# First mixture of experts: the rows of units 4 to 13 by DRAM and indirect gathers that add onto h

## The chip, the cores and the metric

The kernel runs on one core of a Trainium2 chip. The metric is the time of one execution on the device in microseconds, as a median of runs. The profile shows one further execution, taken by the hardware profiler.

## The reference

Two blocks run one after the other on 512 tokens of 1024 numbers in float32. Each is a mixer (two kinds of attention or recurrence side by side), an addition to h, a mixture of experts, and another addition to h. The change lies in the mixture of the first block. Each token chooses one of 4 groups, and 2 of the 8 experts of that group:

```python
def hier_moe(x2d, w_grp, b_grp, w_exp, b_exp, w_gate, w_up, w_down):
    ...
    combine = jnp.sum(jax.nn.one_hot(global_idx, N_EXPERTS, dtype=jnp.float32) * weights[..., None], axis=1)
    y = jnp.zeros_like(x2d)
    for e in range(N_EXPERTS):
        h = jax.nn.silu(x2d @ w_gate[e]) * (x2d @ w_up[e])
        y = y + combine[:, e:e + 1] * (h @ w_down[e])
    return y
...
        h = h + y.reshape(B, S, D)
```

There are 32 experts. `w_gate` and `w_up` are 1024 x 256 each, `w_down` is 256 x 1024: 3 MB an expert in float32.

## The kernel before

**Units.** The first mixture (`moe1`, lines 1626 to 1734) computes only the chosen pairs of token and expert. Each expert has 64 slots; a unit is two experts, 128 slots on 128 partitions, so there are 16 units. The routing, ahead of it, writes the normalised tokens to DRAM (xd) and makes a table of the token number of each slot. For a unit, GpSimd (POOL) gathers the tokens by an indirect transfer (L1579, xg<-xd,idx), TensorE (PE) transposes them (L1592), and multiplies them with the gate and up weights of the two experts: the hidden layer, 64 products that each use half of the columns of PE (L1673). ScalarE (ACT) and VectorE (DVE) make silu(gate) * up, PE transposes that (L1718, `turned`), and the down-projection follows: 16 products (L1641) into two banks of PSUM. ACT and DVE multiply the rows with the slots' weights and split them in a high and a low part (L1738, L1739, `rows_hl`).

**The scatter.** The rows of the slots have to reach the rows of h, which stays in SBUF as four tiles of 128 tokens. Before the change all units do so by products: DVE makes a one-hot matrix of slot and token (L1743), PE multiplies it with the high and the low parts (L1759, L1760: per unit 4 tiles x 2 halves x 2 parts = 16 products), and DVE adds the result onto h (L1753). Two units are summed in PSUM, and their scatter is spread over two later units, half of the columns in each.

**The order.** A unit's down-projection is written after the hidden layer of the next unit. The tile scheduler orders the instructions of each engine ahead of time. After unit 15's hidden layer stands a loop for further rounds (`moe_rounds`, L1572), which handles experts with more than 64 tokens. With these inputs it runs zero times, but its branch is a barrier of all engines, and POOL's and SP's part of it waits until the transfers issued so far have landed. Behind it `end` runs the down-projection of unit 15, its scatter, and `sums_two` (from line 386), the start of the norms of the second block.

**The weights.** SP issues the 96 pieces of 1 MB in the order of use (L1523) into a ring of 17 places of four parts (0 to 3), as places come free. Three of the pieces are issued by POOL.

**Other names.** `places` (L1419) computes where a token's rows stand in DRAM; before the change it is called for the second mixture alone, which sends 14 of its 16 units by a DRAM array yd (stores at L1828) and reads the rows back by plain gathers (L1885). In the first mixer `g` (L470) is a part of the small "lora" weights, `w` the pieces of the input projection (L282), `qz` a tile whose upper half is zero. The mixer goes through steps written out by hand: R for the recurrence, P for projections, A for attention.

## Time and profile before

| what | us |
|---|---|
| runs: lowest, median, highest | 1439.62, 1442.21, 1443.59 |
| span of the profiled execution | 1440.1 |
| PE busy in it | 1329.5 (92%) |
| first mixture, first hidden layer to the last addition onto h | 466.5 to 747.9 |
| the loop's branch on SP | 730.4 |

The page gives the whole execution: busy time by engine, the span in 40 slices, the chain that ended last, and the groups of instructions that cost most. The trace behind it answers for any stretch: which engine was busy, which instruction waited for what, how long a transfer took from issue to landing. The number in front of a row of a timeline is its start, in microseconds from the start of the span.

### The profile page before, as it was taken

Reading aid. Unit: us, or ns where it says so; the run is one execution under the profiler, and the core shown is the slowest. Engines: PE = TensorE matmul, PEld = TensorE weight load, DVE = VectorE, ACT = ScalarE, POOL = GpSimd, SP = SyncE. Lnnn points to the kernel's source line nnn. Section 1 sums busy time; section 2 is a strip of 40 time slices with the busy share of each in tenths; the row PEclk is TensorE's granted clock in tenths of the full one; section 3 lists DMA queues with packets and bytes.
Section 4 is the critical chain, followed back from the end, with each engine's and each line's share of the span. In section 5 each row is a group of like instructions: output and inputs, shape, how many; then the busy total and the mean of one; then the engine's idle time right before and its main releaser. Section 6 shows DMA issues by size and latency. Waiting matters only on the chain. (4 is left out here: it accounts for less than half of the span.)

```text
span 1440.1 us, 20831 instructions
## 1 busy us (share of the span) xinstructions
PE 1329.5 (92%) x7952; PEld 954.6 (66%) x7952; DVE 891.8 (62%) x1498; ACT 700.5 (49%) x1217; POOL 390.2 (27%) x311
## 2 busy tenths in 40 slices
PE   7999999989997999999959899999896999999994
PEld 5776766757696556555528677767795666666662
DVE  4578856575745123323255847565747799999995
ACT  6433433333644212111144555555634788888883
POOL 1010224331104000000047201010223555555555
PEclk9999999999998999999989999999997999999997
DMA  5222100000584999998122111201385899889943
GB/s 186 74 88 74 52 16 1 1 1 2 226 325 166 407 422 422 422 417 346 42 74 72 59 47 57 73 31 34 130 356 199 280 367 373 320 339 395 380 177 147
DMA packets 49286, 273.53 MB, mean 190 GB/s; under 512 B 7497, under 2 KB 8393, under 8 KB 23570
## 3 DMA queue, kind: packets, MB, share of 16 engines
q1 hardware_dynamic: 41058, 249.48, 45.4%
q0 software_dynamic: 7248, 21.24, 4.2%
q10 hardware_dynamic: 864, 1.31, 0.3%
q8 instruction: 66, 1.08, 0.3%
q14 instruction: 50, 0.41, 0.1%
HBM read 266.48 MB, written 11.80 MB: 193 GB/s over the span
## 5 line engine op out<-in xcount | busy, mean ns | idle before, releaser
L1608 DVE TENSOR_TENSOR elo<-ew,ehi 128x1024 fp32r<-128x1024 f32 x147 | 231.3, 1615 | 31.9 <-ACT ehi L1607 23.1
L1607 ACT ACTIVATE ehi<-ew 128x1024 fp32r<-128x1024 f32 x192 | 203.0, 1060 | 61.8 <-PE ua L1855 42.3
L317 PE MATMUL mm<-xh,whi 128*128 128x512 f32 (+1 forms) x384 | 156.6, 408 | 4.0 <-DVE hq L1134 3.7
L317 PE MATMUL mm<-xh,wlo 128*128 128x512 f32 (+1 forms) x384 | 153.3, 399 | 0.0
L317 PE MATMUL mm<-xl,whi 128*128 128x512 f32 (+1 forms) x384 | 152.9, 398 | 0.5 <-DVE xl L349 0.3
L1608 POOL TENSOR_TENSOR elo<-ew,ehi 128x1024 fp32r<-128x1024 f32 x45 | 126.0, 2803 | 63.9 <-ACT ehi L1607 62.2
L1673 PE MATMUL mm<-ew,xTh 128*64 128x256 f32 x1024 | 120.0, 386 | 0.0
L1856 PE MATMUL ua<-elo,xTh 128*96 128x512 f32 x256 | 102.8, 402 | 8.4 <-DVE elo L1608 8.4
L1854 PE MATMUL ua<-ehi,xTh 128*96 128x512 f32 x256 | 101.9, 398 | 0.7 <-ACT xTh L1596 0.6
L1579 POOL DMA_INDIRECT xg<-xd,idx x32 | 36.6, 1145 | 242.7 <-PE sb L1592 153.3
L1855 PE MATMUL ua<-ehi,xTl 128*96 128x512 f32 x256 | 101.6, 397 | 0.0
L1673 PEld LDWEIGHTS mm<-ew,xTh 128*64 128x64 f32 x1024 | 73.6, 139 | 41.9 <-issue 8.0
L291 ACT ACTIVATE whi<-w 128x1024 fp32r<-128x1024 f32 x53 | 55.9, 1056 | 86.7 <-PE mm L317 68.0
L292 DVE TENSOR_TENSOR wlo<-w,whi 128x1024 fp32r<-128x1024 f32 x52 | 64.1, 1234 | 52.4 <-ACT whi L291 51.0
L317 PEld LDWEIGHTS mm<-xh,whi 128*128 128x128 f32 x384 | 73.8, 192 | 23.0 <-DVE hq L1134 5.3
L317 PEld LDWEIGHTS mm<-xl,whi 128*128 128x128 f32 x384 | 73.7, 192 | 16.3 <-issue 3.0
L317 PEld LDWEIGHTS mm<-xh,wlo 128*128 128x128 f32 x384 | 73.4, 191 | 16.3 <-issue 2.6
L1676 ACT ACTIVATE hh<-mm 128x256 f32<-128x256 f32 x16 | 6.1, 383 | 128.9 <-PE mm L1673 128.9
L1677 DVE TENSOR_TENSOR hh<-hh,mm 128x256 f32<-128x256 f32 x16 | 6.7, 421 | 95.1 <-ACT hh L1676 95.1
L1641 PE MATMUL ua<-ew,hT 128*64 128x512 f32 x240 | 65.3, 600 | 0.0
L1856 PEld LDWEIGHTS ua<-elo,xTh 128*96 128x96 f32 x256 | 41.8, 163 | 30.4 <-DVE elo L1608 11.2
L1738 ACT ACTIVATE oh<-ua,wts 128x512 fp32r<-128x512 f32 x30 | 20.6, 687 | 72.9 <-PE ua L1641 72.9
(632 smaller groups left out, 3160.9 us busy)
## 6 DMA issues: line engine op xcount, KB each, us to landing
ew<-in_e1up_dram SPq DMA_DIRECT2D x32, 1024.0 KB, 15.2
ew<-in_e2up_dram SPq DMA_DIRECT2D x32, 1024.0 KB, 11.2
ew<-in_e2gate_dram SPq DMA_DIRECT2D x32, 1024.0 KB, 9.9
ew<-in_e2down_dram SPq DMA_DIRECT2D x32, 1024.0 KB, 11.7
ew<-in_e1gate_dram SPq DMA_DIRECT2D x31, 1024.0 KB, 17.8
ew<-in_e1down_dram SPq DMA_DIRECT2D x30, 1024.0 KB, 16.3
w<-in_win_dram SPq DMA_DIRECT2D x53, 512.0 KB, 3.5
ew<-in_wout_dram SPq DMA_DIRECT2D x8, 1024.0 KB, 7.2
```

Source lines behind the costliest of these rows:

```text
L291: nc.scalar.activation(hi, s, AF.Copy)
L292: (eng or nc.vector).tensor_tensor(lo, s, hi, OP.subtract)
L317: mm = lambda w, x, start=False, stop=False: nc.tensor.matmul(p[:, s], w[:, k], x[:, k, s], start=start, stop=stop, skip_group_check=parts ...
L1579: return self.nc.gpsimd.indirect_dma_start(out=xg, out_offset=None, in_=mo.xd, in_offset=bass.IndirectOffsetOnAxis(ap=idx[:, u:u + 1], axi ...
L1607: self.hi = nc.scalar.activation(hi, s, AF.Copy)
L1608: self.lo = (nc.gpsimd if pool else nc.vector).tensor_tensor(lo, s, hi, OP.subtract)
L1641: nc.tensor.matmul(p[hs(a)], hT[:, k, hs(a)], w[a][:, k * 1024 + d * 512:k * 1024 + d * 512 + 512], start=k == 0, stop=k == 1)
L1673: nc.tensor.matmul(d[hs(a)], xT[:, k, hs(a)], w[2 * m + a][:, k * 256:k * 256 + 256], start=k == 0, stop=k == KD - 1)
L1738: self.last = self.nc.scalar.activation(oh, p, AF.Copy, scale=w)
L1854: nc.tensor.matmul(p, xh[:, kk], hi[:, s], start=kk == 0, stop=False)
L1855: nc.tensor.matmul(p, xl[:, kk], hi[:, s], start=False, stop=False)
L1856: nc.tensor.matmul(p, xh[:, kk], lo[:, s], start=False, stop=kk == KD - 1)
```

## The change

Units 4 to 13 (experts 8 to 27) no longer scatter by products. Their down-projections go through a new function `by_dram`: ACT multiplies the rows with their weights into a tile `ot` (two copies, no split), and POOL stores it by one indirect transfer to `yd`, an array of 1280 rows in DRAM; a slot without a token has a row number out of bounds, and its row is not stored. In unit 14, after unit 13's store, POOL issues eight indirect gathers which add the rows of yd onto h, one for each of the four tiles of tokens and each of a token's two experts (c = 0, 1). Tokens whose expert is not among the twenty have a row number out of bounds. Units 0 to 3 keep the one-hot products in units 3 to 6. Units 14 and 15 keep them too, summed in PSUM in `end` behind the loop: 32 products there instead of 16. `places` is now called in the first mixture as well, and also makes the row numbers of the stores. In step P2 of the first mixer one transfer of SP fills yd with zeros, 5.24 MB in rows of 2 KB. Tags of some tiles are merged, and two of the kept tiles share one place of the ring. In the order of PE, ACT, DVE and POOL in the first mixer some instructions near steps R2, A1 and P2 trade places; their number is the same.

The constants `row` and BYDRAM of the second mixture become `row2` and BYDRAM[2], with the same values. The core of the diff:

```diff
@@ -24,13 +24,16 @@
 SILU = "silu_and_others"
-BYDRAM = 14
-ZROW = BYDRAM * 96
+FROM = {1: 8, 2: 0}
+BYDRAM = {1: 20, 2: 14}
+CAP = {1: 64, 2: 96}
+ZROW = {k: BYDRAM[k] * CAP[k] for k in CAP}
 KAPPA = float(np.exp(-0.5))
@@ -59,8 +62,8 @@
     "mo": (("io64", 64), ("tok", 8), ("upb", 128)),
-    "mo1": (("cap64", 8), ("sl64", 128), ("g_f1", 8)),
-    "mo2": (("cap96", 8), ("sl96", 128), ("g_f2", 8), ("row", 16)),
+    "mo1": (("cap64", 8), ("sl64", 128), ("g_f1", 8), ("row1", 32), ("out1", 16)),
+    "mo2": (("cap96", 8), ("sl96", 128), ("g_f2", 8), ("row2", 16)),
 })
@@ -92,11 +95,13 @@
     put("g_f1", cols(inp["norm_ffn_g"]))
-    put("row", one * np.where(np.arange(16) < BYDRAM, 96 * np.arange(16), 1e5))
+    for k, e in (1, np.arange(32)), (2, np.arange(16)):
+        put("row%d" % k, one * np.where((e >= FROM[k]) & (e < FROM[k] + BYDRAM[k]), CAP[k] * (e - FROM[k]), 1e5))
+    put("out1", i[:, None] + 128 * np.arange(16) - CAP[1] * FROM[1])
     put("g_f2", cols(inp["ffn_norm_2"]))
@@ -487,11 +492,16 @@
                 qkv[j] = self.sb_proj(pp, sp, j, xh, xl)
+                if j == 2:
+                    self.yd = tc.dram_tile([ZROW[1], D], F32, name="yd1")
+                    zeros = qkv[j][0][64:128, 0]
+                    nc.sync.dma_start(self.yd.rearrange("(p a) (d c) -> p (a d) c", p=64, c=T),
+                                      zeros[:, None, :].to_broadcast([64, ZROW[1] // 32, T]))
                 if j == 3:
@@ -1011,10 +1021,9 @@
             self.totals(mo.rp, mo, lb[:, 0:mo.E])
-            if mo.which == 2:
-                self.places(mo.rp, mo)
-
+            self.places(mo.rp, mo)
     def mixer2(self, after):
@@ -1417,22 +1426,29 @@
         nc.vector.tensor_tensor(tm.rearrange("p n c e -> p (n c) e"), mo.M.rearrange("p n c e -> p (n c) e"),
-                                self.c("row")[:, None, :].to_broadcast([128, 2 * NT, E]), OP.mult)
+                                self.c("row%d" % mo.which)[:, None, :].to_broadcast([128, 2 * NT, E]), OP.mult)
         nc.vector.tensor_reduce(rw, tm, AX.X, OP.add)
...
         nc.vector.tensor_tensor(rw, rw, ov, OP.add)
-        nc.vector.tensor_scalar(mo.row, rw, float(ZROW), None, op0=OP.min)
+        if mo.which == 2:
+            nc.vector.tensor_scalar(mo.row, rw, float(ZROW[2]), None, op0=OP.min)
+            return
+        nc.vector.tensor_copy(mo.row, rw)
+        ot = rp.tile([128, mo.U], F32, name="rot")
+        nc.vector.tensor_scalar(ot, mo.num, 4096.0, 1e5, op0=OP.is_ge, op1=OP.mult)
+        nc.vector.tensor_tensor(mo.out, ot, self.c("out1"), OP.add)
 
@@ -1479,7 +1495,8 @@
         mo.extra = mo.keep.tile([1, 1], I32, name="extra")
-        mo.row = mo.keep.tile([128, NT, 2], I32, name="row") if which == 2 else None
+        mo.row = mo.keep.tile([128, NT, 2], I32, name="row")
+        mo.out = mo.keep.tile([128, mo.U], I32, name="out") if which == 1 else None
         self.upb = self.cbf(mo.keep, "upb")
@@ -1630,21 +1647,38 @@
 
-        def down(hT, w, wt, SC):
+        def product(hT, w, d):
+            p = self.ps("dn")
+            for k in range(2):
+                for a in range(2):
+                    nc.tensor.matmul(p[hs(a)], hT[:, k, hs(a)], w[a][:, k * 1024 + d * 512:k * 1024 + d * 512 + 512],
+                                     start=k == 0, stop=k == 1)
+            return p
+        def by_dram(u, hT):
+            w = [self.moe_next(mo) for _ in range(2)]
+            ot = yp.tile([128, D], F32, tag="o1", name="ot", bufs=3)
+            for d in range(2):
+                nc.scalar.activation(ot[:, 512 * d:512 * d + 512], product(hT, w, d), AF.Copy, scale=mo.wts[:, u:u + 1])
+            nc.gpsimd.indirect_dma_start(
+                out=self.yd, out_offset=bass.IndirectOffsetOnAxis(ap=mo.out[:, u:u + 1], axis=0), in_=ot, in_offset=None,
+                bounds_check=ZROW[1] - 1, oob_is_err=False)
+        def down(hT, w, wt, SC, at=None):
             hl = []
             for d in range(2):
-                hl.append([yp.tile([128, 512], R32, name=nm + str(d), bufs=2 + d) for nm in ("oh", "ol")])
-                p = self.ps("dn")
-                for k in range(2):
-                    for a in range(2):
-                        nc.tensor.matmul(p[hs(a)], hT[:, k, hs(a)], w[a][:, k * 1024 + d * 512:k * 1024 + d * 512 + 512],
-                                         start=k == 0, stop=k == 1)
-                self.rows_hl(*hl[d], p, wt)
+                y = at[:, d] if at is not None else yp.tile([128, 2, 512], R32, tag="o%d" % d, name="oh%d" % d, bufs=2 + d)
+                hl.append([y[:, 0], y[:, 1]])
+                self.rows_hl(*hl[d], product(hT, w, d), wt)
             return SC, hl
...
             ys, prev = [], None
+            far = range(FROM[1] // 2, (FROM[1] + BYDRAM[1]) // 2) if first else ()
             for u in range(2):
@@ -1661,7 +1695,11 @@
                 last = u == mo.U - 1
-                if last:
+                if last and first:
+                    SC = self.place(mo, 2, R32)
+                    y14 = down(prev[1], [self.moe_next(mo) for _ in range(2)], wts[:, u - 1:u], onehot(u - 1, SC[:, 0:T]),
+                               self.place(mo, 2, R32).rearrange("p (d i c) -> p d i c", d=2, i=2))
+                elif last:
                     self.scatter(ys[12:14], 0)
@@ -1678,30 +1716,39 @@
                 nx = self.gathered(gp, xgs[(u + 1) % 2], False)
-                if u > 2:
-                    e = (u - 3) // 2 * 2
+                e = (u - 3) // 2 * 2
+                if e >= 0 and (not first or e < far[0]):
                     self.scatter(ys[e:e + 2], (u + 1) % 2)
-                if prev:
+                if prev and prev[0] in far:
+                    by_dram(*prev)
+                elif prev:
                     ys.append(down(*down_args(*prev, num, wts)))
+                if far and u == far[-1] + 1:
+                    for c in range(2):
+                        for n in range(NT):
+                            nc.gpsimd.indirect_dma_start(
+                                out=self.h[:, n], out_offset=None, in_=self.yd,
+                                in_offset=bass.IndirectOffsetOnAxis(ap=mo.row[:, n, c:c + 1], axis=0),
+                                bounds_check=ZROW[1] - 1, oob_is_err=False, compute_op=OP.add)
                 hT = gp.tile([128, 2, 128], F32, name="hT", bufs=1)
...
                 prev = u, hT
-            self.scatter(ys[12:15], 1)
-            self.scatter(ys[14:15], 0)
             if not first:
+                self.scatter(ys[12:15], 1)
+                self.scatter(ys[14:15], 0)
                 hT = gp.tile([128, 2, 128], F32, name="hT", bufs=1)
                 turned(hh, hT)
-                return first, *down_args(mo.U - 1, hT, num, wts)
-            keep, SC, gs = self.place(mo, 2), self.place(mo, 2, R32)[:, 0:T], self.place(mo, 3)
+                return first, None, *down_args(mo.U - 1, hT, num, wts)
+            keep, gs = self.place(mo, 2), self.place(mo, 3)
             hT, wt = keep[:, 0:256].rearrange("p (k t) -> p k t", k=2), keep[:, 256:257]
             nc.vector.tensor_copy(wt, wts[:, mo.U - 1:mo.U])
-            onehot(mo.U - 1, SC)
+            SC = onehot(mo.U - 1, SC[:, T:2 * T])
             turned(hh, hT)
             w = [self.moe_next(mo) for _ in range(2)]
-            raw, hl = self.place(mo, 2)[:, 0:D], self.place(mo, 3, R32).rearrange("p (i k c) -> p i k c", i=2, k=KD)
+            raw, hl = keep[:, D:2 * D], self.place(mo, 3, R32).rearrange("p (i k c) -> p i k c", i=2, k=KD)
             nc.sync.dma_start(raw, self.ap["win2"][4])
@@ -1710,7 +1757,7 @@
                 nc.sync.dma_start(t, self.ap[nm].to_broadcast([128, D]))
-            return first, hT, w, wt, SC
+            return first, y14, hT, w, wt, SC
 
@@ -1718,33 +1765,33 @@
 
-        def end(first, *args):
+        def end(first, y14, *args):
             if first:
...
                 self.ordered.enter_context(self.in_order())
-            y = down(*args)
+            ys = ([y14] if first else []) + [down(*args)]
             if first:
...
                 for d in range(2):
-                    self.scatter([y], d, [n], ("so", "gu", "so", "dn"))
+                    self.scatter(ys, d, [n], ("so", "gu", "so", "dn"))
```

The instructions of PE from the down-projection in unit 7 to the next hidden layer; before, with the last scatter products of that unit ahead of it (oh, ol: rows in high and low part; SC: one-hot matrix; ua: bank of the down-projection; sb: bank of the transposes):

```order
L1760 MATMUL pq<-ol_4954,SC 128x512
L1759 MATMUL pq<-oh_5066,SC 128x512
L1760 MATMUL pq<-ol_5067,SC 128x512
L1641 MATMUL ua<-ew_5173,hT 64x512
L1641 MATMUL ua<-ew_5175,hT 64x512
L1641 MATMUL ua<-ew_5173,hT 64x512
L1641 MATMUL ua<-ew_5175,hT 64x512
L1641 MATMUL ua<-ew_5173,hT 64x512
L1641 MATMUL ua<-ew_5175,hT 64x512
L1641 MATMUL ua<-ew_5173,hT 64x512
L1641 MATMUL ua<-ew_5175,hT 64x512
L1718 MATMUL sb<-pc_c,hh 128x128 x2
```

The same place after, from the last product of the hidden layer on:

```order
L1711 MATMUL mm<-ew_5098,xTh 64x256
L1609 MATMUL sb<-pc_c,xg_4404 128x128 x8
L1655 MATMUL ua<-ew_5149,hT 64x512
L1655 MATMUL ua<-ew_5151,hT 64x512
L1655 MATMUL ua<-ew_5149,hT 64x512
L1655 MATMUL ua<-ew_5151,hT 64x512
L1655 MATMUL ua<-ew_5149,hT 64x512
L1655 MATMUL ua<-ew_5151,hT 64x512
L1655 MATMUL ua<-ew_5149,hT 64x512
L1655 MATMUL ua<-ew_5151,hT 64x512
L1765 MATMUL sb<-pc_c,hh 128x128 x2
L1711 MATMUL mm<-ew_5177,xTh 64x256
```

The sixteen scatter products between the transposes of the gathered tokens (there L1592, here L1609) and the down-projection (L1641, here L1655) are gone; the rest stands as it was. The transposes of hh are L1718 and L1765, the hidden products L1673 and L1711.

The down-projection that stands in unit 9 on PE, before:

```order
L1641 MATMUL ua<-ew_5399,hT 64x512
L1641 MATMUL ua<-ew_5401,hT 64x512
L1641 MATMUL ua<-ew_5399,hT 64x512
L1641 MATMUL ua<-ew_5401,hT 64x512
L1641 MATMUL ua<-ew_5399,hT 64x512
L1641 MATMUL ua<-ew_5401,hT 64x512
L1641 MATMUL ua<-ew_5399,hT 64x512
L1641 MATMUL ua<-ew_5401,hT 64x512
L1718 MATMUL sb<-pc_c,hh 128x128 x2
```

and after:

```order
L1655 MATMUL ua<-ew_5319,hT 64x512 x2
L1765 MATMUL sb<-pc_c,hh 128x128 x2
L1609 MATMUL sb<-pc_c,xg_4405 128x128 x4
L1655 MATMUL ua<-ew_5321,hT 64x512
L1655 MATMUL ua<-ew_5319,hT 64x512
L1655 MATMUL ua<-ew_5321,hT 64x512 x2
L1655 MATMUL ua<-ew_5319,hT 64x512
L1655 MATMUL ua<-ew_5321,hT 64x512
L1609 MATMUL sb<-pc_c,xg_4405 128x128 x4
```

The products of the two experts (two ew tiles) alternated from the start; now two of the first expert stand ahead, then the transposes of hh and four of the next unit's, then the others. In the order before, that pattern begins two units later.

On POOL, the instructions from the last gathers of tokens to the branch of the loop, with the semaphores they wait for (DMASW: landings of POOL's own transfers), before:

```order
L1579 DMA xg_4388<-xd_3852,idx 128x1024 [waits DMASW7_49,PE_49]
L1579 DMA xg_4389<-xd_3852,idx 128x1024 [waits DMASW0_49,PE_49]
L1571 TENSOR_LOAD extra [waits DVE_49,Activation_49,Pool_49]
L1572 COMPARE_AND_BRANCH
L1572 ISA [waits DMASW4_49,DMASW5_49,DMASW3_49,DMASW6_49,DMASW2_49,DMASW7_49,DMASW1_49,DMASW0_49]
L1572 UNCONDITIONAL_BRANCH
L1572 ISA [waits barrier_Pool_Activation_PE_DVE_SP_gather]
L1572 UNCONDITIONAL_BRANCH [waits barrier_Pool_Activation_PE_DVE_SP_gather]
```

and after, from the last store (unit 13's) on:

```order
L1665 DMA yd_2625<-ot,out 1280x1024 [waits DMASW3_49,Activation_49]
L1730 DMA h<-yd_2625,row 128x1024 [waits DMASW4_49,DVE_49]
L1730 DMA h<-yd_2625,row 128x1024 [waits DMASW6_49,DVE_49]
L1730 DMA h<-yd_2625,row 128x1024 [waits DVE_49]
L1730 DMA h<-yd_2625,row 128x1024 [waits DMASW0_49,DVE_49]
L1730 DMA h<-yd_2625,row 128x1024 [waits DMASW5_49]
L1730 DMA h<-yd_2625,row 128x1024 [waits DMASW6_49]
L1730 DMA h<-yd_2625,row 128x1024 [waits DMASW7_49]
L1730 DMA h<-yd_2625,row 128x1024 [waits DMASW0_49]
L1588 TENSOR_LOAD extra [waits DVE_49,Activation_49,Pool_49]
L1589 COMPARE_AND_BRANCH
L1589 ISA [waits DMASW4_49,DMASW5_49,DMASW3_49,DMASW6_49,DMASW2_49,DMASW7_49,DMASW1_49,DMASW0_49]
```

Ahead of the branch there are now the eight gathers onto h. The first waits for a landing (DMASW4, the last store's), the last four for the landings of the first four (DMASW5, 6, 7, 0), and the branch's ISA row, as before, for all landings.

## Rows read from the trace of the kernel before

**Rows 1.** Page, 40 slices of 36 us: busy tenths of PE, GB/s.

```profile
PE   7999999989997999999959899999896999999994
GB/s 186 74 88 74 52 16 1 1 1 2 226 325 166 407 422 422 422 417 346 42 74 72 59 47 57 73 31 34 130 356 199 280 367 373 320 339 395 380 177 147
```

**Rows 2.** Table by stretch: first mixture, and one of the first mixer.

```profile
core 0: us, PE busy (x) PEld busy (x) DVE busy (x) ACT busy (x) POOL busy (x), PEclk, DMA share, GB/s
464.00:684.00 220.00, 218.87 (x1427) 126.99 (x1428) 61.86 (x103) 41.91 (x81) 14.30 (x15) 0.98 0.99 405
501.00:612.00 111.00, 111.00 (x744) 65.67 (x742) 34.81 (x55) 21.82 (x42) 6.92 (x7) 1.00 1.01 422
684.00:730.00 46.00, 45.01 (x238) 23.53 (x236) 14.70 (x25) 6.84 (x13) 0.00 (x0) 1.00 0.10 34
180.00:220.00 40.00, 38.66 (x341) 26.95 (x340) 24.38 (x50) 15.58 (x31) 13.74 (x23) 1.00 0.04 15
```

**Rows 3.** SP's waits, 370 to 760: us in total, times, longest us.

```profile
SPq L1523 <- PE mm L1673: 106.7, 28, 11.0
```

**Rows 4.** Timeline of PE, first mixture: start us, us, line, tiles, count.

```profile
489.43 7.13 PE L1673 MATMUL mm<-ew,xTh 128*64 128x256 f32 x64
501.46 7.13 PE L1673 MATMUL mm<-ew,xTh 128*64 128x256 f32 x64
564.91 7.13 PE L1673 MATMUL mm<-ew,xTh 128*64 128x256 f32 x64
576.83 3.65 PE L1641 MATMUL ua<-ew,hT 128*64 128x512 f32 x16
580.78 7.13 PE L1673 MATMUL mm<-ew,xTh 128*64 128x256 f32 x64
697.85 1.88 PE L1641 MATMUL ua<-ew,hT 128*64 128x512 f32 x4
700.03 3.65 PE L1641 MATMUL ua<-ew,hT 128*64 128x512 f32 x12
735.27 6.24 PE L1641 MATMUL ua<-ew,ew 128*64 128x512 f32 x16 [5.63 <-DMA ew<-in_attn_g_dram]
741.44 0.50 PE L1759 MATMUL ch<-oh,ew 128*128 128x512 f32 x1
745.99 0.39 PE L1760 MATMUL ua<-ol,ew 128*128 128x512 f32 x1
```

**Rows 5.** Chain that ended last, 690 to 760: start us, us, what.

```profile
730.41 0.02 SPq L1572
731.11 4.14 DMA ew<-in_attn_g_dram
746.62 1.28 DVE h L1753 x2
```

**Rows 6.** Lines 1885, 1828, 1579 in turn: issue ns, us to landing.

```profile
L1885 POOL DMA_INDIRECT ew<-yd,row x8: 990/1321/7542, 1392.1 to 1409.3; - x8
DMA to landing us min/median/max: 5.2/5.5/5.6
...
DMA to landing us min/median/max: 3.0/7.3/8.1
...
L1579 POOL DMA_INDIRECT xg<-xd,idx x32: 971/1009/1780, 460.2 to 1343.7; - x32
DMA to landing us min/median/max: 4.3/8.2/10.1
```

**Rows 7.** SP's timeline and line 852: load and first use of g.

```profile
167.38 0.33 SPq L470 DMA_DIRECT2D g<-in_lora_dram  x1
...
L852 PE MATMUL ua<-xg,g x32: 272/275/276, 203.1 to 359.8; 128*128 128x128 f32 x32
```

**Rows 8.** Timelines of POOL and DVE, end of the second mixture.

```profile
1395.41 7.54 POOL L1885 DMA_INDIRECT ew<-yd,row  x1 [0.30 <-DVE ew L1739]
...
1395.20 8.10 DVE L1608 TENSOR_TENSOR elo<-ew,ehi 128x1024 fp32r<-128x1024 f32 x7
```

8 lines of the change are left out of this document (4 added, 4 removed).

## The prediction

> **What bounds the kernel now.** I read the page first: of its 40 slices of 36 us the fourteenth to the twentieth (468 to 720 us) show PE at 9 throughout, while GB/s runs at 407 to 422, then 346, then 42 [rows 1]. This is the first mixture, and the table by stage comes next. From 464 to 684 both are full: PE 218.87 of 220 us, DMA share 0.99 at 405 GB/s. From 684 to 730 PE is still full (45.01 of 46) but DMA is at 0.10 [rows 2]. The weights are all there by about 684, and PE needs 46 us more. In the waits, SP, which issues the weights, stood 106.7 us waiting for PE's hidden products to free places of the ring [rows 3]: PE paces the stage, but the stream of weights has almost no slack. Both limits are needed below.
>
> What PE does in that stage is read off its timeline. Hidden layers without scatter start 12.03 us apart (489.43 to 501.46), with scatter 15.87 (564.91 to 580.78) [rows 4]. The difference, 3.84 us, is the 16 scatter products of a unit. In the late units the scheduler puts four products of the down-projection ahead: these four take 1.88 us and the other twelve 3.65, as long as sixteen in the usual order (row at 576.83), so a late unit is 1.9 us longer [rows 4].
>
> The stage ends at a barrier of all engines, the branch of the loop for further rounds, which I call the door. SP goes through it at 730.4; behind it come the attn_g load (landed at 735.25), the down-projection of unit 15, and its scatter [rows 5]. The after-door part is a fixed chain, so the time follows the door.
>
> **PE's part.** Before the door 240 scatter products become 64: 176 go, eleven times 3.84, 42 us of PE. Units 3 to 6 still scatter, so unit 7's hidden layer starts at 564.9 as now. Units 7 and 8 then take 12.03 each: unit 9 at 589.0. Units 9 to 14 take 12.03 + 1.9 = 13.9 each, since the order puts four products first from unit 9 on: 672.4. Unit 14's own down-projection follows, 3.65: unit 15's hidden layer starts at 676.0, takes 7.1, and its activation and transposes some 2: PE would be at the door at **685**.
>
> **The weights' part.** The stream cannot be faster than full. By 684 it has moved 220 us x 405 GB/s = 89.1 MB; its best long stretch is 422 GB/s [rows 2]. The change adds the stores: 1024 pairs of token and expert, 20 of 32 experts, so about 640 rows of 4 KB, 2.6 MB, 6 us at 422. If the old stream lost nothing to PE, it now ends at 690; if all its distance to 422 was lost to PE (89.1 MB + 2.6 MB at 422: 217 us), at 681. I take **687**, nearer the first, since the first slices are slow for another reason (the stream starts there). SP's side of the door waits for every load, so this is a floor of the door; PE and the stream are level, and a still leaner PE would bring nothing.
>
> **The gathers' part.** This is new, and ends last. In POOL's order after the last store stand eight indirect gathers that add onto h; the first waits for the last store (unit 13's), the fifth to eighth for the first to fourth of the same tile, and the loop's branch on POOL for all of them to land.
> - Unit 13's down-projection lies in unit 14 (658.5 to 672.4 by the sum above), behind its hidden layer; its weights are about the sixth- to seventh-last pieces of the stream, six at 2.5 us (1 MB at 422) before 687. Both give 672. ACT's copy takes it to 672.8.
> - Store: the nearest rows are the second mixture's, where a direct store lands 3.0 to 8.1 us after its issue [rows 6]. Under a full stream I take the upper end, 8.1: first gather at **681**.
> - Issue: the plain gathers of the second mixture hold POOL 1.0 to 1.3 us each (median 1321 ns) [rows 6]: four of them 681 to 686, the last issued at 684.9.
> - Landing: plain gathers land 5.2 to 5.6 us after issue where the queues are calm (128 rows, 0.52 MB), gathers of xg under the stream 4.3 to 10.1, median 8.2 [rows 6]. The trace has no accumulating transfer; it moves fewer rows here (1024 x 20/32 over eight, 80 of 128, 0.33 MB), but reads its destination too. Bounds: 5.2, as if plain and calm, and 16.4, twice the loaded median. I take 8.2, the loaded row, since the stream ends only at 687 and the reads of h come on top. First four landed at 689.2 to 693.1; second four issued as these land; last landed 693.1 + 8.2 = **701.3**, door about **702**.
>
> The Trainium skill, page "DMA: Bandwidth & Descriptors", section "Anatomy of one DMA — SWDGE (gpsimd) path", gives 2.0 us and the bytes at 436 GB/s for a transfer issued by GpSimd. By an estimate from it the 80 rows would land in 2.8 us, the door would be at 681 + 3.9 + 5.6 = 690.5, and the time near 1405. The trace disagrees: the calm 0.52 MB gathers took 5.5 us, the formula gives 3.2.
>
> So the door moves from 730.4 to 702: **-28.4**.
>
> **Behind the door.** Units 14 and 15 are summed there: 32 products in place of 16. Now the sixteen start from 741.44 to 745.99, with a stall in between; without one a product takes 3.84 / 16 = 0.24 us [rows 4]. The additions of VectorE set the pace now, the last two in 1.28, ending at 747.9 [rows 5]. With four products a bank (0.96) PE sets it: 741.44 + 32 x 0.24 = 749.1, last addition, 0.64 longer, at 749.8: **+1.9**. PE idles longer ahead of the door than its 5.63 us now; the sixteen down products after that pause took 6.24 us instead of 3.65 [rows 4]. Should PE's clock stay at its low level into the new products (twice the pitch), this costs up to 3.8 more; that goes into the range.
>
> **Ahead of the stage.** `places` adds some nine small VectorE operations beside the routing chain: between 0, if POOL and PE are waited for anyway, and 1.5; taken **+0.5**. The twenty ACT copies replace copies of the same size, the subtractions that go were hidden. The zero fill of yd (5.24 MB) stands ahead of the g load on SP, which now leaves at 167.4; g is first used at 203.1 [rows 7]. DMA is nearly idle there (15 GB/s, share 0.04) [rows 2]. At 422 GB/s the fill takes 12.4 us, at half of that 25: g lands by 196, and is in time by 7 us. Cost 0; with that cover gone, each us of lateness is one of PE. The reshuffled order there leaves the same products to PE.
>
> **Sum.** -28.4 + 1.9 + 0.5 = -26.0. The profiled span of 1440.1 becomes 1414.1. The median of the runs, 1442.2, is 2.1 above that span; so **1416** us.
>
> **Rivals.**
> 1. *Gathers cheap, the stream is the bound.* Stores land in 3.0, gathers in 5.2: 672.8 + 0.5 + 3.0 + 3.9 + 5.2 + 5.2 = 690.6, level with the stream's 687 to 690. Door 690: -40.4 + 2.4, and 1404. For it: fewer rows than 128. Against: the queues are full until about 687.
> 2. *Gather-adds run one after the other, or at half rate.* Eight landings of 5.5 in a row end at 725: -5.4 + 2.4, 1439, no difference. At half rate (landing 16.4, twice): 681 + 3.9 + 32.8 = 718, 1432. For it: nothing in the trace accumulates, and each packet has a destination to read. Against: the plain ones overlap (issue every 1.3, landing 5.5).
> 3. *Slower: POOL is held at each issue.* One of the eight plain gathers held POOL 7.54 us, from 1395.41, while VectorE ran seven subtractions back to back from 1395.20 [rows 8]. If that is the price of each new issue, the last is issued at 681 + 60.3 and the door is at 747: +16.6 + 2.4, **1461**. It decides from 5.2 us an issue on (681 + 8 x 5.2 + 5.5 = 728). Against: VectorE has little between 681 and 702, and the median of the eight is 1.3. The Trainium skill, page "SBUF — State Buffer", section "SBUF: two separate sides", says that a VectorE operation that takes the port shared with GpSimd locks out the writing of descriptors for as long as it runs, which agrees with that 7.54 us row; by it the time depends on VectorE alone, and this rival on its having work then.
> 4. *The zero fill is slow* (a quarter of the full rate: 50 us from about 165), so that g lands near 218, 15 us after its first use at 203.1: 1416 + 15 = 1431. Against: nothing else is on the queues there, and the pieces are 2 KB, not small.
>
> **Chances.** Forecast (door 694 to 712, 1408 to 1426) 0.57; rival 1 0.15; rival 2 0.13, half of it within 0.3% of now; rival 3 0.09; rival 4 0.06. A difference under about 0.3%, 4.3 us, cannot be told from none. Faster: 0.57 + 0.15 + 0.07 + 0.06 = 0.85; same 0.06; slower 0.09. The range takes in rival 1 and the doubled landing of rival 2: 1402 to 1432, which leaves out rival 3, the serial half of rival 2 and a little beyond both ends, some 0.18.
>
> **What would show it.** Hidden layers from unit 7 on about 12, then 14 us apart (or 15, if PE waits for weights: then the stream rules); hidden layer of unit 15 starting near 676; DMA busy until 687; the first gather-add issued near 681; the door near 702 with POOL's transfers the last to land, and PE idle ahead of it for some 15 us. Wrong it would be by a door at 690 with the gathers landed before (rival 1), landings beyond 10 us (rival 2), gather issues of more than 2 us (rival 3), or a wait of PE in 200 to 260 us (rival 4). The weakest number is the landing of an accumulating gather: it enters twice, so a us there moves the time by two.

## The result, and the profile after

The changed kernel takes 1422.0 us in the median (1419.7 to 1423.1) against 1441.9 for the kernel before in the same set: a ratio of 0.986, 95% interval 0.985 to 0.988, 20 us faster. The forecast was 1416, range 1402 to 1432. Its profiled execution spans 1417.9 us; that of before spanned 1440.1.

The line numbers after: hidden layer L1711, down-projection L1655, `turned` L1765, store L1665, gathers that add L1730, scatter products L1806 and L1807, their additions onto h L1800, the loop's branch L1589, loads behind the door L1759, zero fill L503, g L475.

Page of the kernel after, 40 slices of 35 us: busy tenths of PE, GB/s (answers [rows 1]).

```profile
PE   7999999999897999999379999999996999999993
GB/s 189 75 89 75 107 109 2 1 1 2 188 330 170 386 419 419 418 418 422 223 101 75 30 76 45 86 24 100 105 334 209 321 360 382 320 332 391 385 166 125
```

Before, a slice of full PE with 42 GB/s stood at the end of the stage; now the twentieth slice has PE at 3 and 223 GB/s. The table by stretch says what that is (columns as in [rows 2]).

```profile
464.00:684.00 220.00, 213.62 (x1447) 117.77 (x1448) 27.63 (x50) 47.43 (x91) 24.41 (x25) 0.99 1.01 414
692.00:707.00 15.00, 0.00 (x0) 0.00 (x0) 0.00 (x0) 0.00 (x0) 6.21 (x4) 0.55 0.78 131
```

The 46 us in which PE worked alone are gone, but for 15 us at the end no engine but POOL does anything, the DMA engines are busy to 0.78 of the time and move only 131 GB/s. PE's granted clock falls to its lower level meanwhile (0.50 from 696 on). The timeline of POOL shows what they move (start us, us, instruction, [idle before <- releaser]).

```profile
675.07 0.97 POOL L1665 DMA_INDIRECT yd<-ot,out  x1 [14.87 <-ACT hT L1766]
683.70 1.63 POOL L1730 DMA_INDIRECT h<-yd,row  x1 [7.65 <-DMA yd<-ot,out]
685.64 1.59 POOL L1730 DMA_INDIRECT h<-yd,row  x1 [0.31 <-issue]
692.49 1.55 POOL L1730 DMA_INDIRECT h<-yd,row  x1 [1.53 <-DMA h<-yd,row]
698.78 1.55 POOL L1730 DMA_INDIRECT h<-yd,row  x1 [0.31 <-issue]
```

The last store leaves at 675.1, its landing releases the first gather, the landings of the first four release the fifth and sixth, and the eighth is issued at 698.8. The chain that ended last runs through them to 707.0, and the door follows. (The last gather itself has landed at 705.8; the rest up to 707.0 is POOL's part of the branch.) The median landing is in the list of DMA issues.

```profile
687.53 19.46 DMA h<-yd,row
707.00 1.62 issue
708.62 6.25 PE ua L1655 x16
...
h<-yd,row POOLq DMA_INDIRECT x8, 7.8
```

PE on its timeline: the hidden layers of units 10 to 13 start 13.7 us apart (unit 12 at 628.78, unit 13 at 642.51); in units 13 to 15 half a layer waits for weights.

```profile
615.04 7.13 PE L1711 MATMUL mm<-ew,xTh 128*64 128x256 f32 x64
628.78 7.13 PE L1711 MATMUL mm<-ew,xTh 128*64 128x256 f32 x64
648.50 3.67 PE L1711 MATMUL mm<-ew,xTh 128*64 128x256 f32 x30 [1.63 <-DMA ew<-in_e1up_dram]
664.61 3.67 PE L1711 MATMUL mm<-ew,xTh 128*64 128x256 f32 x30 [1.62 <-DMA ew<-in_e1up_dram]
678.61 0.59 PE L1711 MATMUL mm<-ew,xTh 128*64 128x256 f32 x2
685.99 3.67 PE L1711 MATMUL mm<-ew,xTh 128*64 128x256 f32 x30 [1.43 <-DMA ew<-in_e1up_dram]
690.58 0.44 PE L1765 MATMUL sb<-pc_c,hh 128*128 128x128 f32 x2 [0.93 <-DVE hh L1715]
708.62 6.25 PE L1655 MATMUL ua<-ew,ew 128*64 128x512 f32 x16 [17.60 <-issue]
```

PE arrives at the door at 691.0 and stands there for 17.6 us. In what follows each execution is counted from its own first hidden layer (466.5 before, 464.0 after), because that point varies by 4 us between executions of these kernels, and "PE restarts" is the start of unit 15's down-projection behind the door. The first layer itself is not equally long in all executions, here in the changed kernel and in e1_no_adds:

```profile
463.97 9.16 PE L1711 MATMUL mm<-ew,xTh 128*64 128x256 f32 x64
```

```profile
466.93 7.54 PE L1711 MATMUL mm<-ew,xTh 128*64 128x256 f32 x64
```

The granted clock is 0.50 from 462 to 466 in both and 0.73 and 0.77 from 466 to 470, so the changed kernel's layer, which starts 3 us earlier, runs longer at the lower clock. The second count, from the start of the second hidden layer, leaves that out: by it the two profiles of the kernel before agree within 0.2 us (257.9 and 257.7), by the first they are 1.2 apart. Differences between kernels are therefore taken from the second count below. Each is one profiled execution.

| kernel | PE restarts, us after the first hidden layer | after the second | PE stood, us | median of runs, or single run |
|---|---|---|---|---|
| before | 268.8 | 257.9 | 5.6 | 1441.9 |
| changed | 244.7 | 233.9 | 17.6 | 1422.0 |
| e1_no_adds | 232.6 | 223.4 | 5.8 | 1409.2 (single) |
| e3_first_four | 235.8 | 225.9 | 8.7 | 1413.9 (single) |
| e2_plain | 240.0 | 230.2 | 12.8 | 1415.0 (single) |
| e8_no_stores | 223.8 | 213.0 | 5.7 | 1400.8 (single) |
| e5_units_4_11 | 246.6 | 236.8 | 6.0 | 1423.3 |
| e6_plain_and_add | 247.4 | 237.4 | 20.6 | 1423.7 |
| e7_plain_zeroed | 242.7 | 232.8 | 15.5 | 1418.4 |
| e10_adds_behind_4 | 236.3 | 226.7 | 8.7 | 1417.6 |
| e11_adds_behind | 239.0 | 229.3 | 11.2 | 1415.8 |

### The profile page after: what moved, and what is told of

It is laid out like the page before. It is cut to its first block, busy times and chain, and to the rows that moved or that the text cites. A ratio compares the mean times of both kernels' runs of the same rounds, so it can differ in the third digit from the quotient of the medians.

```text
span 1417.9 us, 20482 instructions
## 1 busy us (share of the span) xinstructions
PE 1289.0 (91%) x7792; PEld 927.7 (65%) x7792; DVE 841.6 (59%) x1432; ACT 701.6 (49%) x1217; POOL 410.2 (29%) x329
## 4 chain that ended last, share of the span: by engine, by line
PE 68%; DVE 13%; DMA 11%; ACT 3%; issue 2%; POOL 1%; SPq 0%; DVEq 0%; POOLq 0%; ACTq 0%
PE mm L322 12%; PE ua L1903 4%; PE ua L1901 4%; PE ua L1902 4%; PE mm L1711 4%; DMA ew<-in_e1down_dram 3%; DMA ew<-in_e1up_dram 3%; PE ua L1655 2%; PE sb L322 2%; PE sb L1844 2%; PE sb L1843 2%; PE sb L1845 2%; PE sb L715 2%; DMA ew<-in_e1gate_dram 2%; DVE elo L1625 2%
## 5 line engine op out<-in xcount | busy, mean ns | idle before, releaser
L1711 PE MATMUL mm<-ew,xTh 128*64 128x256 f32 x1024 | 119.2, 386 | 6.4 <-DMA ew<-in_e1up_dram 4.7
L1711 PEld LDWEIGHTS mm<-ew,xTh 128*64 128x64 f32 x1024 | 73.5, 139 | 47.5 <-DMA ew<-in_e1up_dram 6.4
L1655 PE MATMUL ua<-ew,hT 128*64 128x512 f32 x240 | 66.4, 600 | 1.2 <-ACT hT L1766 1.1
L1903 PEld LDWEIGHTS ua<-elo,xTh 128*96 128x96 f32 x256 | 41.9, 164 | 30.6 <-DVE elo L1625 11.2
L1167 POOL TENSOR_TENSOR hAT<-hAT,hmt 128x512 f32<-128x512 f32 x16 | 22.1, 1381 | 118.9 <-DVE hmt L1166 118.3
## 6 DMA issues: line engine op xcount, KB each, us to landing
ew<-in_e1down_dram SPq DMA_DIRECT2D x30, 1024.0 KB, 20.6
```

The source lines that it names most:

```text
L1655: nc.tensor.matmul(p[hs(a)], hT[:, k, hs(a)], w[a][:, k * 1024 + d * 512:k * 1024 + d * 512 + 512], start=k == 0, stop=k == 1)
L1711: nc.tensor.matmul(d[hs(a)], xT[:, k, hs(a)], w[2 * m + a][:, k * 256:k * 256 + 256], start=k == 0, stop=k == KD - 1)
L1903: nc.tensor.matmul(p, xh[:, kk], lo[:, s], start=False, stop=kk == KD - 1)
```

## The experiments

**Without the eight gathers** (the rows of units 4 to 13 never reach h):

```diff
-                if far and u == far[-1] + 1:
+                if False:
```

> Leaves out the eight gathers that add the rows of units 4 to 13 onto h (the stores stay); the output lacks those rows. It shows the loop's branch (the door) without them, and what PE does behind the door. Stage theory: PE's last transposes ended at 691.0 in the changed kernel and the weights had landed by about 690, so the door comes at 692 instead of 707. Behind the door there are two readings of why PE restarted 0.7 us after SP in the changed kernel, and 4.6 us after SP before. If PE's code behind the branch is loaded only when PE has stood idle at it, PE comes back 4 to 5 us after the door here, as before, and the span is some 1417.9 - 12 = 1406; if the difference came from the attn_g load or the other code, PE restarts within 1 us and the span is 1402 to 1403.

PE restarts 10.5 us earlier than in the changed kernel (223.4 for 233.9). It stood 5.8 us all the same; PE's two rows, and one of SP:

```profile
693.25 0.44 PE L1765 MATMUL sb<-pc_c,hh 128*128 128x128 f32 x2 [0.93 <-DVE hh L1715]
699.48 1.97 PE L1655 MATMUL ua<-ew,ew 128*64 128x512 f32 x4 [5.79 <-issue]
699.61 0.66 SPq L1759 DMA_DIRECT2D ew<-in_attn_g_dram  x1
```

Of the two readings on record the first came near: it had PE back 4 to 5 us after a door at 692 and a span of 1406; measured are 699.5 and 1407.4. The second, a restart within 1 us of that door, is out. SP too passes only at 699.2. The loop's branch costs 5.5 to 6.0 us from PE's arrival wherever nothing else is later: 5.6 before, 5.8 here, 5.7 and 6.0 in two kernels below. Of the 17.6 us that PE stands in the changed kernel, 11.8 belong to the gathers.

**The stores left out too** (neither stores nor gathers):

```diff
-            nc.gpsimd.indirect_dma_start(
-                out=self.yd, out_offset=bass.IndirectOffsetOnAxis(ap=mo.out[:, u:u + 1], axis=0), in_=ot, ...
```

> Leaves out the stores to DRAM and the gather-adds, so units 4 to 13 never reach h: what is left is the removal of the products. It prices the stores, which the prediction put at 2.6 MB, 6 us of the stream of weights. Counted from the first hidden layer, the kernel without the adds alone had its door at 232.3 and unit 15's hidden layer at 216.6. If the stores cost the stream 6 us, unit 15's hidden layer starts 5 to 6 us earlier and the door stands near 226; if PE and the waits for places of the ring pace the late units, it moves by less than 2 us.

```profile
676.85 7.13 PE L1708 MATMUL mm<-ew,xTh 128*64 128x256 f32 x64
691.06 1.98 PE L1655 MATMUL ua<-ew,ew 128*64 128x512 f32 x4 [5.72 <-issue]
```

Unit 15's hidden layer starts at 676.9 and runs without a break, so PE is never short of weights here, and it restarts 10.3 us earlier than with the stores (213.0 for 223.4 in e1_no_adds; 8.8 by the first count). PE arrives at the branch 10.3 us earlier than in e1_no_adds and 8.9 earlier than in the changed kernel. 2.6 MB of stores in a stream that is full cost 9 to 10 us at the door, where their bytes alone at 422 GB/s would be 6.

**The first four gathers alone** (each token's first expert only):

```diff
-                    for c in range(2):
+                    for c in range(1):
```

> Leaves out the second four gather-adds (the tokens' second expert). Throughput theory: half of the bytes, so the DMA engines are done 8 us earlier: last issue at 225.4 from the first hidden layer, landed near 234, door 235 to 236. Latency theory: the second round costs a whole landing and four issues in series, from 225.4 + 1.6 to 234.8, 9 us, so the door comes at 234 to 235. The two differ little here; the run shows how long four landings last when nothing follows: above 8 us for the last of them speaks for the transfer rate, 5 to 6 for latency and queueing of the second four.

PE restarts at 225.9: 2.5 later than with no gather, 8.0 earlier than with eight. The second four are the dear ones; the first four lie mostly beside the end of the weights and beside the 5.8 us of the branch.

**Plain gathers in place of gathers that add** (h is overwritten):

```diff
-                                bounds_check=ZROW[1] - 1, oob_is_err=False, compute_op=OP.add)
+                                bounds_check=ZROW[1] - 1, oob_is_err=False)
```

> The same eight gathers, rows, indices and waits, but copying over h instead of adding (so h loses what was there in those rows). Only the accumulation goes. Throughput theory (an adding gather moves at about 160 GB/s with the DMA engines full, and this sets the last 16 us): landings fall to 5 to 6 us and the GB/s of the stretch behind the weights rises towards 340, the door comes at 700 to 701, 6 to 7 us earlier. Latency theory (store, issue at 1.87 us each and two landings in series set it, whatever the rate): landings stay near 8, door 706 to 707.

```profile
687.20 1.03 POOL L1730 DMA_INDIRECT h<-yd,row  x1 [7.54 <-DMA yd<-ot,out]
688.54 1.00 POOL L1730 DMA_INDIRECT h<-yd,row  x1 [0.31 <-issue]
695.09 0.99 POOL L1730 DMA_INDIRECT h<-yd,row  x1 [2.96 <-DMA h<-yd,row]
699.74 0.99 POOL L1730 DMA_INDIRECT h<-yd,row  x1 [0.30 <-issue]
...
h<-yd,row POOLq DMA_INDIRECT x8, 4.8
```

Landings of the last four gathers, in the changed kernel and here:

```profile
DMA to landing us min/median/max: 6.3/6.7/7.3
```

```profile
DMA to landing us min/median/max: 3.9/4.4/4.9
```

An issue holds POOL 1.0 us instead of 1.55, and the pitch is 1.3 instead of 1.9. The last four land after 3.9 to 4.9 us instead of 6.3 to 7.3. (The median of 4.8 is not to be held against 7.8: it leaves out two of the first four, whose landings the profile does not tell; the other two took 6.9 and 8.0, beside the end of the weights.) PE restarts 3.7 us earlier (230.2 for 233.9). That lies between the two theories: the adding itself costs 3.7, and 6.8 are left of what the gathers cost over e1_no_adds; they go with the chain of two landings behind a store, which this run keeps.

**Everything earlier: units 4 to 11 only,** so that the last store and the gathers lie under the stream. Units 12 and 13 get their one-hot products back, ahead of unit 15's hidden layer:

```diff
-BYDRAM = {1: 20, 2: 14}
+BYDRAM = {1: 16, 2: 14}
...
+                if last and first:
+                    self.scatter(ys[4:6], 0)
+                    self.scatter(ys[4:6], 1)
```

> By DRAM only units 4 to 11, so that the eight adding gathers start two units earlier, at about 651, under the stream of weights; units 12 and 13 scatter by products ahead of unit 15's hidden layer (32 products more before the door, in PE's waits for weights). Output complete. Throughput theory: the gathers' 2.1 MB at 160 GB/s take 13 us of the DMA engines wherever they run, so the weights end some 8 us later, near 698, and the door comes at 700 to 702, 5 to 7 us earlier than in the changed kernel. Latency theory: the chain is hidden under the stream, the weights end at 690 as now, the door comes at 692 to 695.

The gathers are issued from 653.4 to 675.5, and PE gets to the door at 706.9, long after the landings; yet the door is no earlier. The table by stretch of this kernel, then of the changed one:

```profile
658.00:676.00 18.00, 14.61 (x85) 7.37 (x82) 2.71 (x5) 2.52 (x5) 7.46 (x6) 0.91 1.04 351
676.00:692.00 16.00, 14.56 (x49) 5.63 (x48) 4.19 (x7) 3.03 (x5) 1.07 (x1) 1.00 0.98 351
...
h<-yd,row POOLq DMA_INDIRECT x8, 16.4
```

```profile
658.00:676.00 18.00, 15.22 (x91) 7.27 (x91) 0.80 (x3) 3.48 (x7) 1.90 (x2) 1.00 1.01 420
```

The DMA engines are as busy as before (1.04), but they move 351 GB/s in place of 420: the gathers that add take engine time out of proportion to their bytes. The weights come later: the second half of unit 14's layer, which waits for them, starts at 669.37, 193.3 us after the second hidden layer, against 189.8 in the changed kernel. Who waited for whom from 676 to 714 shows another price (us in total, times, longest):

```profile
DVE h L1803 <- DMA h<-yd,row: 9.2, 3, 3.9
PE pq L1809 <- DVE h L1803: 3.5, 2, 2.6
```

The additions of the one-hot products onto h have to wait for the gathers that add onto the same tile, and PE waits 3.5 us for those additions. The 32 products themselves take PE about 10 us, the last twelve 4.4 of them with the granted clock at 0.60 (694 to 698). These, more than the weights, are why PE arrives at the branch 14.6 us later than in the changed kernel (230.8 for 216.3). All but two products of unit 15's hidden layer start at 698.5, PE stands its 6.0 us at the branch, and nothing is won (1423.3, ratio 0.989, 0.986 to 0.992). So the run shows that the gathers lower the rate of a full stream, but it does not price them alone: it brings the products back as well, and lets them collide with the gathers on h.

**Plain gathers beside each other, added by DVE.** Eight gathers go into four free places of the ring, zeroed ahead, so none waits for another; DVE adds them onto h:

```diff
+            ys2 = [self.place(mo, 0) for _ in range(NT)]
+            for y in ys2:
+                nc.vector.memset(y, 0.0)
...
-                                out=self.h[:, n], ... compute_op=OP.add)
+                        out=ys2[n][:, D * c:D * c + D], ...)
+            for c in range(2):
+                for n in range(NT):
+                    nc.vector.tensor_tensor(self.h[:, n], self.h[:, n], ys2[n][:, D * c:D * c + D], OP.add)
```

> The eight gathers copy into four places of the ring that no later weights use (set to zero by VectorE before), without a wait of the second four for the first, and VectorE adds them onto h with eight operations of 1.2 us. Output complete. Throughput theory: 2.6 MB at 340 to 400 GB/s, last landed 697 to 699, door near 700: 7 us earlier than in the changed kernel, about 1411 by its profile. Latency theory: only the wait between the first and second four goes, last issue near 697, landing 8, door near 706.

It missed: PE restarts at 247.4, 1423.7 us. The zeroing of two of the places stood behind unit 15's work in DVE's order, the fifth gather waited 4.6 us for it, and its issue and the next, beside DVE's zeroing and additions, took 3.3 and 2.0 us. So the same once more with the zeroing on POOL while it waits for the store anyway, and the last weights issued ahead:

```diff
+                    mo.ahead += [self.moe_load(mo) for _ in range(8 - len(mo.ahead))]
...
-                nc.vector.memset(y, 0.0)
+                        nc.gpsimd.memset(y, 0.0)
```

> As the plain gathers into the ring with additions by VectorE, but GpSimd sets the four places to zero while it waits for the last store, and the last weights are issued ahead of it in the program. Output complete. Counted from the start of the first hidden layer, the changed kernel's door is at 244.0 and its first gather-add at 219.7. Throughput theory: plain gathers issue every 1.3 us without a wait between the fours, the last at 229, landed by 235; VectorE's additions follow the landings, eight of 1.23: the last ends at 237 to 238. Door 238, PE back at 239, 5 to 6 us earlier than in the changed kernel: about 1416. Latency theory: landings stay near 8 and the door near 241 to 242: 1419 to 1420. Against both: VectorE's additions and the issue of gathers hold each other up (3.3 us an issue where they met in the version with late zeroing).

All eight are issued between 687.2 and 696.3, one every 1.3 us. What this says of the adding is in the DMA queues, first of the changed kernel (684 to 707), then of this one (684 to 712): packets, MB, share of 16 engines.

```profile
q0 software_dynamic: 1152, 2.58, 69.5%
```

```profile
q0 software_dynamic: 1232, 2.62, 26.8%
```

For the same bytes the queue of POOL takes 0.695 x 23 = 16.0 us of all sixteen engines where the gathers add, and 0.268 x 28 = 7.5 where they copy: twice the time a byte. PE restarts at 242.7, not the expected 239, and 1 us earlier than in the changed kernel (by the second count; 1418.4, ratio 0.983, 0.982 to 0.985): the bound is now DVE, whose last addition ends at 709.4, 0.5 us before PE restarts.

**The additions moved behind the door:** three of the eight beside unit 15's down-projection, or four:

```diff
+            for n in range(NT):
+                nc.vector.tensor_tensor(self.h[:, n], self.h[:, n], ys2[n][:, 0:D], OP.add)
+            nc.vector.tensor_tensor(self.h[:, 3], self.h[:, 3], ys2[3][:, D:2 * D], OP.add)
...
         def end(first, y14, *args):
+                for n in range(3):
+                    nc.vector.tensor_tensor(self.h[:, n], self.h[:, n], self.late[n][:, D:2 * D], OP.add)
```

> As in e7_plain_zeroed (plain gathers into four zeroed places of the ring, added onto h by DVE), but of the eight additions of DVE only five stand ahead of the door; three stand behind it, beside unit 15's down-projection. Theory, that in e7_plain_zeroed the door waited for DVE's additions alone: its gathers had all landed by 702.8 and the additions ended at 709.4. With five ahead the door comes one addition (1.2 us) after the last landing, near 704, so 237 us after the first hidden layer in place of 242.7; the three others take 3.7 us of DVE, which has nothing else until unit 15's rows, 5 us behind the door. Time near 1413. Rival, that DVE's additions are slowed by other work at that place (in e7_plain_zeroed they took 1.6 us in the mean, the longest 3.4, beside two operations of POOL that stay where they are): the five end near 707, door at 240, 1416; the three behind then hold up unit 15's rows: 1418, no gain over e7_plain_zeroed.

The timelines of POOL and DVE:

```profile
697.33 2.41 POOL L1763 TENSOR_TENSOR ew<-ew,ew 128x1024 fp32r<-128x1024 f32 x1 [0.83 <-issue]
699.71 3.31 POOL L402 TENSOR_TENSOR ew<-ew 128x1024 f32<-128x1024 f32 x1
...
696.32 1.23 DVE L1755 TENSOR_TENSOR h<-h,ew 128x1024 f32<-128x1024 f32 x1 [0.68 <-DMA ew<-yd,row]
698.39 5.71 DVE L1755 TENSOR_TENSOR h<-h,ew 128x1024 f32<-128x1024 f32 x2 [0.85 <-DMA ew<-yd,row]
704.13 1.23 DVE L1756 TENSOR_TENSOR h<-h,ew 128x1024 f32<-128x1024 f32 x1
707.42 3.50 DVE L1781 TENSOR_TENSOR h<-h,ew 128x1024 f32<-128x1024 f32 x3 [2.06 <-issue]
```

The two additions that lie beside POOL's operations take 5.7 us together, the others 1.2 each; that is 3.3 us of the door, as the rival said, and PE restarts at 239.0 between the two theories. The three behind the door cost nothing: the last addition onto h ends 14.6 us after PE restarts, as in the changed kernel. With 1415.8 us (1414.6 to 1416.7; ratio 0.983, 0.981 to 0.985) this has the lowest median of the kernels here that compute all: 25 us below the one before of its own set, where the changed kernel is 20 below. That it is faster than e7_plain_zeroed and e10_adds_behind_4 is not shown, since the intervals of their ratios overlap.

> As e11_adds_behind, but four additions of DVE stand ahead of the door and four behind, and with them the last two gathers and two operations of POOL go behind the door as well. Theory: the door waits for six gathers, of which the sixth is issued at 693.7 and lands 6.5 later, near 700.5, and for four additions that end near 702: 235 us after the first hidden layer. PE cannot restart before 700, 5.7 us after its arrival. Behind the door the last two gathers are issued at 703 and land near 708, the last addition ends near 710.5 and holds up the low part of unit 15's rows (needed at 708.5) by 2 to 3 us. Sum: 7.5 earlier at the door than e7_plain_zeroed, 2 to 3 given back behind it: 1413 to 1414. Rival: new code or POOL's issue behind the door costs as much as the two gathers saved (the gathers are issued 3 us later and land at 711): 1416 to 1418.

With four behind, the last two gathers and the two operations of POOL go there too. PE restarts earlier, at 236.3, but one addition takes 5.2 us beside POOL's operations, the low part of unit 15's rows starts at 714.7 in place of 710.8, and the median is 1417.6 (1413.5 to 1420.1). That is the rival's time, and in part its cause: the last gather lands at 711.1 as it said, but the slow addition, which runs from 708.5 to 713.7, ends later still.

**The kernel before once more.**

> The kernel before once more, for a second profile. In the first pair of profiles the first hidden layer started 2.5 us earlier in the changed kernel, and the stretch after the last store to the output was 2.2 us longer. If these belong to the change, this profile repeats the first one: hidden layer at 466.5, last output issued 9.8 us ahead of the end. If they are differences between executions, it is off by 1 us or more in either.

Its first hidden layer starts at 467.6 (466.5 in the other profile) and PE restarts at 267.6 (268.8). Over all these kernels the start lies between 464.0 and 468.4, so the 2.5 us by which the changed kernel's profile starts earlier is no effect of the change. From the last output's issue to the end of the span it is 9.8 and 10.3 us in the two profiles of before, and 10.7 to 12.1 in the profiles of the changed kernel and its variants. What makes it longer was not found.

## Why the prediction was right, and where its terms were off

The counts of this section are from the first hidden layer, as the forecast has them; that layer took 9.3 us before, 9.2 in the changed kernel and 9.1 in e8_no_stores, so these three can be compared.

**What PE sheds: right.** By the forecast PE, left to itself, would start unit 15's hidden layer at 676.0, 209.5 us after its first one, and be at the door at 685, 218.5 after it. Where nothing else is in the way, without stores and gathers, it does so at 209.5 (676.85 - 467.31) and stands at the door at 218.0 (691.06 - 5.72 - 467.31).

**The weights and the stores: too small.** The forecast took the bytes of the stores at the full rate and put unit 13's rows at 672.8, 206.3 us after the first hidden layer. The store leaves at 675.07, 211.1 after it: **+4.8**. The stream was not simply longer by its bytes. With the stores PE runs short of weights from unit 13 on (its second half waits 1.6 us at 648.50), which the section on what would show each step had as a possibility ("then the stream rules"), and PE's own way to the door grows by 9 to 10 us, not 6. The last piece of weights, issued at 670.45, lands 21.6 us later at 692.0, 228.1 after the first hidden layer, where the forecast had the stream end at 220.5.

**The store's landing: right.** 8.1 us were taken, and the gather starts 8.6 after the store's issue (683.70 - 675.07): +0.4.

**The issue of the gathers: too small.** 1.3 us a gather came from the plain ones of [rows 6]. A gather that adds holds POOL 1.55 us and the pitch is 1.9. From the first to the last issue it is 15.1 us (698.78 - 683.70) where the forecast had 12.1: **+3.0**. Of this 1.7 is the pitch. The other 1.2 are the landings of the first two, for which the fifth and the sixth wait: these start 8.8 and 9.4 us after the first and the second, where the forecast had 8.2. That adding makes the issue dearer is shown by e2_plain, where everything else is the same.

**The landing: near in size, for another reason.** 8.2 was taken from the gathers of xg under the stream, on the grounds that the stream would still run. The median is 7.8, and the last takes 7.0 (698.78 to 705.8): **-1.2**. But no stream runs then (the queue of the weights moves 0.03 MB from 692 to 707): the last four plain gathers of e2_plain land after 3.9 to 4.9 at the same place, the adding ones after 6.3 to 7.3. It is the adding, which the forecast named as its weakest number, that makes up the difference, so the nearness of the number was luck. Rival 2 (half rate) was right in its mechanism, twice the engine time per byte, and wrong in its size, since 16.4 us a landing appear only under the stream (e5_units_4_11). Rival 1 (gathers cheap) was wrong on both counts. The Trainium skill, page "DMA: Bandwidth & Descriptors", section "Anatomy of one DMA — SWDGE (gpsimd) path", would by an estimate have the 80 rows land in 2.8 us; the last four plain ones took 3.9 to 4.9, the last four adding ones 6.3 to 7.3.

**The door.** From the last landing to SP's passing it is 2.2 us (705.8 to 707.93), where the forecast had 0.7: **+1.5**. The sum of these (4.8 + 0.4 + 3.0 - 1.2 + 1.5) is 8.5. SP passes the door 244.0 us after the first hidden layer, where 702 would have been 235.5: 8.5 later.

**Behind the door: one term misread, to the good.** The forecast kept the 4.14 us of the attn_g load ahead of PE's restart, as the chain of before has it [rows 5]. But in the changed kernel PE restarts 0.7 us after SP has passed, while that load is still under way:

```profile
707.93 0.34 SPq L1759 DMA_DIRECT2D ew<-in_fin_g_dram  x1
708.33 0.56 SPq L1759 DMA_DIRECT2D ew<-in_attn_g_dram  x1
```

So the attn_g load was not what PE waited for, although the trace of before names it as the releaser [rows 4]. In e1_no_adds PE stands just as long and restarts at 699.48, before the load is issued at 699.61. And before the change, PE restarts at 735.27, when the load has not landed: POOL, which needs it, is held until 736.39.

```profile
736.39 2.34 POOL L397 TENSOR_TENSOR ew<-ew 128x1024 f32<-128x1024 f32 x1 [0.84 <-DMA ew<-in_attn_g_dram]
```

What fits every profile is that PE takes 5.5 to 6.0 us from its arrival at the branch, and this now lies inside the 17.6 us that it stands anyway. That gives back **4.2** us (4.56 from SP's passing to PE's restart before, 0.69 after; the forecast had 4.85). PE's own queue at the branch shows where they go (min/median/max ns of one, first and last start in us), before, after and in e1_no_adds:

```profile
L1572 PEldq COMPARE_BRANCH  x3: 104/193/3489, 729.8 to 735.0; - x3
```

```profile
L1589 PEldq COMPARE_BRANCH  x3: 100/190/5383, 691.7 to 708.4; - x3
```

```profile
L1589 PEldq COMPARE_BRANCH  x3: 104/193/3504, 694.0 to 699.2; - x3
```

One branch instruction of the three takes 3.5 us before and in e1_no_adds, and 5.4 in the changed kernel, where PE's wait covers it; the rest are checks of semaphores and the two short branches. What fills the long branch was not settled. The DMA queues marked "instruction" carry packets in just that time (five between 731 and 736 before, PE having arrived at 729.6; seven between 694 and 699 in e1_no_adds, arrival 693.7), which points to code behind the branch being fetched; but no run changed it.

**The products of units 14 and 15: right.** +1.9 was forecast. From PE's restart to the end of the last addition it was 12.63 us (735.27 to 747.90) and is 14.62 (708.62 to 723.24): +2.0. The pause did not add to it beyond that: the down products take 6.25 us as in [rows 4].

**The zero fill: right.** It lands in 28.3 us at 205 GB/s, half of the full rate, the slower of the two rates that the forecast named. The g load behind it, issued at 165.1, lands 27.7 us later at 192.8, and g is first used at 208.5. PE does not wait for it. Rival 4 is out.

**POOL held at its issues (rival 3): right to leave it small.** No issue took over 1.63 us, since DVE has little to do there. Its mechanism is real, and came into play as soon as experiments put DVE's work beside the gathers: issues of 3.3 and 2.0 us in e6_plain_and_add.

**The sum.** PE's restart came 24.1 us earlier, counted from the first hidden layer (268.8 to 244.7). By the forecast's terms it was to be 28.4, so the balance is 8.5 lost and 4.2 won back. That the time came as near as it did is in part luck: two errors of opposite sign, one in the chain to the door, one in the wait behind it. Of the span, 22.2 were gained for 26.0 forecast: 4.3 less by the restart, 2.5 less from the last addition to the end (692.2 us before, 694.7 after; most of it the longer tail above), and 2.5 more by the earlier start, which is chance. The half microsecond for `places` cannot be told within that. The median of the runs moved by 19.9; the profiled execution of the changed kernel was its fastest run (1419.7).

## What to carry to other kernels

When a change takes work off an engine that is level with a stream, look at the chain that the change itself adds at the end: here 45 us of PE were taken out and 21 came back, about 10 through the stores in a full stream and about 10.5 through the gathers behind them. A transfer that adds onto its destination is to be priced apart from a plain one, in issue and in engine time, and it is worth asking whether independent plain transfers and additions on an idle engine, placed where nothing waits for them, do the same. A wait that the trace puts down to a transfer that ends at about that time can be another wait; an execution in which the two come apart settles it. And a point from which executions are counted should be one where they agree: here the second hidden layer, not the first.

## What the runs showed of the hardware that had not been expected

- **Gathers that add** (0.33 MB each): 1.55 us of POOL at issue, 6.3 to 7.3 us to landing behind the stream, 152 to 177 GB/s with the DMA engines busy to 0.89 and more (688 to 704); the plain ones 1.0 at issue, 3.9 to 4.9 to landing at the same place. Under the stream of weights those that add land after 16.4 us, and the total rate is 351 GB/s in place of 420.
- **The loop's branch** costs PE 5.5 to 6.0 us from its arrival, with a loop that runs zero times; one branch instruction of its queue is 3.3 to 3.7 of them.
- **DVE and POOL hold each other up.** An addition on DVE with both inputs in SBUF takes 1.2 us alone, and 3.4 or 5.2 beside two-input operations of POOL. The Trainium skill, page "SBUF — State Buffer", section "SBUF: two separate sides", says that such operations take the pair of ports that the two engines share for the whole instruction and that the other waits; these numbers agree. In e10_adds_behind_4 a gather's issue took 2.05 us in place of 0.99 beside such additions (in the trace of before one took 7.54 beside DVE's subtractions, [rows 8]): the issue can be held up as well. Where it starts decides: this one started at 705.84, while DVE was adding, and ended 0.87 us after the additions did (707.89 and 707.02); in e7_plain_zeroed one that started at 694.99, just ahead of an addition at 695.21, took its 0.99.
